# Weight stream of a 32-expert layer: order of the low part's products, place of the down biases, one more raw buffer

## The chip, the core and the metric

One core of a Trainium2 chip runs the whole program. The metric is the device time of one execution in microseconds (us), the median of several runs. The engines have their own instruction queues: PE (TensorE, matrix products), DVE (VectorE), ACT (ScalarE), POOL (GpSimd, here mostly the issuer of indirect transfers) and SP (SyncE, the issuer of the weight loads). An instruction waits for semaphores at the head of its engine's queue, and what stands behind it waits with it.

## The reference

512 tokens of width 1024 pass through a first block (retention and pooling, an expert layer, an embedding gate) and a second block of attention. The change touches the expert layer alone:

```python
def moe(hn, router_w, router_b, w_gu, b_gu, w_down, b_down):
    logits = xt @ router_w + router_b
    top_vals, top_idx = lax.top_k(logits, TOP_K)
    gates = jax.nn.softmax(top_vals, axis=-1)
    ...
    gu = lax.ragged_dot(xs, w_gu, group_sizes) + b_gu[sorted_e]
    gate = jnp.minimum(gu[:, ::2], SWIGLU_LIMIT)
    up = jnp.clip(gu[:, 1::2], -SWIGLU_LIMIT, SWIGLU_LIMIT)
    act = (up + 1.0) * (gate * jax.nn.sigmoid(SWIGLU_ALPHA * gate))
    y = lax.ragged_dot(act, w_down, group_sizes) + b_down[sorted_e]
    y = y * gates[order]
    out = jnp.zeros_like(xt).at[tok].add(y)
```

Everything is in fp32. The weights of an expert are 1024x2048 (gate and up) and 1024x1024 (down), 12 MB, 384 MB for all 32: each is read once.

## The kernel before

**Precision.** A product in fp32 is made of products of a coarser type, fp32r. A weight tile is split in a high part (`wh`, a copy on ACT, L937) and a low part (`wl`, raw minus high, on DVE, L938). The token matrix is split likewise (`xh`, `xl`). The product is xh·wh + xl·wh + xh·wl.

**Tiles.** `chunks` walks an expert's three 1024x1024 matrices (the gate_up halves 0 and 1, down) in row tiles of 128x1024: 8 for a matrix, 24 for an expert, 768 in all. One load of 1 MB, issued by SP through `load` (L167), brings two tiles into the next raw buffer of the ring `self.wr`: `wr` (2 buffers), `wr2` (3) and two halves of the residual's buffer `self.h`, seven in all. A load waits until the two tiles that the buffer held have been split. Six pairs of buffers hold high and low parts in turn (`parts`).

**Two kinds of experts.** Sixteen experts (0, 1, 3, 5, ... 29) have room for 96 tokens, and xh and xl are separate operands: six matmuls of 96 rows by 512 columns a tile, in the helper `mm3` (L187 xh·wh, L188 xl·wh, L189 xh·wl), first for the bank of columns 0 to 511, then for that of 512 to 1023. The other sixteen (2, 4, ... 30, 31) have room for 64, and xh and xl stand side by side in one operand of 128 columns: four matmuls a tile (L942). The diff leaves these as they are. The two kinds are streams of their own (`stream`), which the loop at the end of `moe` takes in turn, a tile of each, once the stream of the first kind has a lead of 24 tiles; so the last 24 tiles are of the second kind alone.

**Side work.** What isn't a product of weights runs as jobs: generators that are stepped between tiles, each saying after how many tiles it wants its next step. `fetch` gathers an expert's tokens (POOL, `xg`) and transposes them, `clamped` and `folded` apply the activation, `out` scales the result (ACT, `ys`) and adds it to `y_d` in memory by an indirect transfer of POOL (L1028). All additions into `y_d` come one after the other, each when the one before has landed. `finish` runs a job to its end at once where its result is needed. Jobs share two PSUM banks named `tr`; `bank()` hands them out.

**The down biases.** `gated_bias` adds gates times `b_down` to all 512 tokens, 128 at a time (t = 0 to 3): a transpose of the gates, two matmuls of 512 columns, two copies on ACT into `yb` (L1148), and an indirect addition of 512 KB into `y_d` (L1150). Its job starts at the many-token expert 11. There is one buffer `yb`, which the raw bias rows (`bd`) use first.

**The start.** `early` issues the first loads before the router's tables are ready: seven into the ring, then, behind the branch that deals with overflowing experts (`overflow`), an eighth into the result buffer `ys`. After the last tile, `y_d` is read back (L1265) and the embedding gate follows, then the attention block.

Of the kernel before, what the change touches and what calls it, by code (L numbers as in the profile page):

```python
# [9 lines left out]
F32 = mybir.dt.float32  # L10
F32R = mybir.dt.float32r
# [3 lines left out]
AF = mybir.ActivationFunctionType  # L15
ALU = mybir.AluOpType
# [3 lines left out]
D = 1024  # L20
# [122 lines left out]
class Kern:  # L143
# [189 lines left out]
    def run(self):  # L333
        tc, nc, I = self.tc, self.nc, self.I
        with ExitStack() as g:
            self.con = g.enter_context(tc.tile_pool(name="con", bufs=1))
            self.dr = g.enter_context(tc.tile_pool(name="dr", bufs=1, space=bass.MemoryType.DRAM))
            self.h = self.con.tile([128, NT, D], F32, name="h")
            self.hn_d = self.dr.tile([S, D], F32, name="hn_d")
            self.y_d = self.dr.tile([S, D], F32, name="y_d")  # L340
            self.x2_d = self.dr.tile([S, D], F32, name="x2_d")
            wr = g.enter_context(tc.tile_pool(name="wr", bufs=2))
            wh = g.enter_context(tc.tile_pool(name="wh", bufs=2))
            with ExitStack() as a:
                wr2 = a.enter_context(tc.tile_pool(name="wr2", bufs=3))
                self.wr = [wr2, wr, wr2, wr, wr2]
                self.wh = [wh] * 2
                self.rp = a.enter_context(tc.tile_pool(name="rp", bufs=1))
                self.junk = self.rp.tile([128, D], BF16, name="junk")
                with ExitStack() as f:  # L350
                    self.front(f)
                with ExitStack() as f:
                    Q = f.enter_context(tc.tile_pool(name="mq", bufs=2, reuse_waits="tile"))
                    self.wr = [wr, wr2, wr, wr2, wr2] + [Part(self.h[:, 2 * i:2 * i + 2, :]) for i in range(2)]
                    self.moe(f, Q)
                self.wr, self.wh = [wr], [wh]
            with ExitStack() as f:
                self.back(f)
# [449 lines left out]
    def moe(self, f, Q):  # L808
# [115 lines left out]
        def chunks(src, ps, pair, raw=(), bias=None, few=False):  # L924


            if bias is not None and not few:
                for n in range(2):
                    bias(n, True)
            for c0 in range(0, 8, 2):  # L930
                w = raw.pop(0) if raw else self.load(src(c0 * 128, 256).rearrange("o (k p) n -> p (o k) n", p=128), 2, 1024)
                for kk in range(2):
                    k = c0 + kk
                    hi, lo = self.next(parts)
                    if raw:
                        nc.vector.tensor_copy(hi[:, 0:1], tabs[0][1])
                    nc.scalar.activation(hi, w[:, kk], AF.Copy)  # L937
                    nc.vector.tensor_tensor(out=lo, in0=w[:, kk], in1=hi.bitcast(F32), op=ALU.subtract)  # L938
                    if few:
                        for part in (hi, lo):  # L940
                            for n in range(2):
                                nc.tensor.matmul(ps[:, n, :], pair[2][:, k, :], part[:, n * 512:n * 512 + 512],  # L942
                                                 start=k == 0 and part is hi, stop=k == 7 and part is lo)
                                if bias is not None and k == 0 and part is hi:
                                    bias(n, False)
                    else:
                        for n in range(2):
                            nn = slice(n * 512, n * 512 + 512)
                            self.mm3(ps[:, n, :], (pair[0][:, k, :], pair[1][:, k, :]), (hi[:, nn], lo[:, nn]),
                                     bias is None and k == 0, k == 7)  # L950
                    yield k

        def pieces(src, ps, pair, first, last):
# [162 lines left out]

        def gated_bias():

            bd = T.tile([128, D], F32, tag="yb", name="bd", bufs=1)
            for r in range(0, 128, NE):  # L1120
                nc.sync.dma_start(bd[r:r + NE], I["expert_b_down"][0])
            bs = P.tile([128, D], F32R, name="bs")
            yield 8
            nc.scalar.activation(bs, bd, AF.Copy)
            nc.vector.tensor_tensor(out=bs[64:128], in0=bd[64:128], in1=bs[64:128].bitcast(F32), op=ALU.subtract)
            rows = P.tile([128, NT], I32, name="rows")
            for t in range(NT):
                g4 = T.tile([128, 4, NE], F32, tag="g4", name="g4", bufs=1)
                nc.vector.tensor_copy(g4, self.G[:, t, None, :].to_broadcast([128, 4, NE]))
                nc.vector.tensor_scalar(rows[:, t:t + 1], c["far"], 128.0 * t - FAR - 1, None, op0=ALU.add)  # L1130
                yield 1
                tp, free = yield from bank()
                nc.tensor.transpose(tp[:, 0:128], g4.rearrange("p a e -> p (a e)"), c["ident"])
                yield LAG
                gT = T.tile([128, 128], F32R, tag="gT", name="gT", bufs=1)
                nc.scalar.activation(gT, tp[:, 0:128], AF.Copy)
                yield 1
                for r in (32, 96):
                    q = slice(r, r + NE)
                    nc.vector.tensor_tensor(out=gT[q], in0=tp[q, 0:128], in1=gT[q].bitcast(F32), op=ALU.subtract)  # L1140
                free()
                yield 1
                y = T.tile([128, D], F32, tag="yb", name="yb", bufs=1)
                for n in range(2):
                    ps, free = yield from bank()
                    nc.tensor.matmul(ps, gT, bs[:, n * 512:n * 512 + 512], start=True, stop=True)
                    yield LAG
                    nc.scalar.activation(y[:, n * 512:n * 512 + 512], ps, AF.Copy)  # L1148
                    free()
                nc.gpsimd.indirect_dma_start(out=self.y_d[:, :], out_offset=bass.IndirectOffsetOnAxis(ap=rows[:, t:t + 1], axis=0),  # L1150
                                             in_=y, in_offset=None, bounds_check=S - 1, oob_is_err=False, compute_op=ALU.add)
                yield 8

        ne = self.ne
        self.gates(self.G[:, :, 0:2], self.tcols0, 2, T)
# [11 lines left out]
            nc.sync.dma_start(dst, self.wsrc(wgu[i // 8], 2 * (i % 4), 2, 1024 * (i // 4 % 2), 1024))  # L1167
            return dst

        raws = [early(i, self.next(self.wr).tile([128, 2, 1024], F32, tag="wr", name="wr")) for i in range(7)]  # L1170
        overflow()
        raws.append(early(7, ys))

        def stream(es):

            for e, after in zip(es, es[1:] + [None]):
# [2 lines left out]
                    J[after, "x"] = job(fetch(after, 16))  # L1179
                if not LESS[e] and 4 * (at // 2) + 4 in BATCHES and at % 2 == 0:  # L1180
                    job(table(4 * (at // 2) + 4))
                if e == 11:
                    job(gated_bias())
                yield from gate_up(e, 0)
                if at and after is not None:
                    yield from down(es[at - 1])
                yield from gate_up(e, 1)
            for e in es[-2:]:
                yield from down(e)
# [494 lines left out]
```

## Time and profile before

| | |
|---|---|
| median of 3 runs | 1834.57 us (1832.08 to 1838.57) |
| profiled run | 1836.86 us |
| its span, first to last instruction | 1835.0 us |
| mean granted clock of TensorE | 0.981 of full speed |
| busy share of the span | PE 95%, DVE 83%, ACT 65%, POOL 12% |
| weights and other data read | 470.90 MB |

The profile is one execution. Its stages: up to about 250 us the first block's mixing, the router and the tables; to about 1362 us the expert stream; then the embedding gate and the attention. Busy times of PE are modelled and overlap, so a busy PE is not one at its peak. The DMA share is the mean busy share of the 16 DMA engines, and it can pass 1.00 a little. The granted clock is TensorE's, as a share of 2.4 GHz; its two levels are 1.2 and 2.4.

### The profile page before, as it was taken

Reading aid. Unit: us, or ns where it says so; the run is one execution under the profiler, and the core shown is the slowest. Engines: PE = TensorE matmul, PEld = TensorE weight load, DVE = VectorE, ACT = ScalarE, POOL = GpSimd, SP = SyncE. Lnnn points to the kernel's source line nnn. Section 1 sums busy time; section 2 is a strip of 40 time slices with the busy share of each in tenths; the row PEclk is TensorE's granted clock in tenths of the full one; section 3 lists DMA queues with packets and bytes.
Section 4 is the critical chain, followed back from the end, with each engine's and each line's share of the span. In section 5 each row is a group of like instructions: output and inputs, shape, how many; then the busy total and the mean of one; then the engine's idle time right before and its main releaser. Section 6 shows DMA issues by size and latency. Waiting matters only on the chain. (4 is left out here: it accounts for less than half of the span.)

```text
span 1835.0 us, 24671 instructions
## 1 busy us (share of the span) xinstructions
PE 1739.8 (95%) x8375; PEld 1285.0 (70%) x8379; DVE 1529.2 (83%) x2665; ACT 1193.9 (65%) x1591; POOL 221.2 (12%) x124
## 2 busy tenths in 40 slices
PE   8999779999999998999999999999978999999999
PEld 6887657666776775766666666766656777787776
DVE  5574589999999998999999999999977769999542
ACT  5224258778878777887788788788875445554431
POOL 0011212131111311210201211110310000000000
PEclk9999879999999998999999999999999999999999
DMA  8224469999999999999999999999985222201211
GB/s 283 85 95 149 147 219 354 384 354 389 378 391 386 373 379 363 341 391 383 379 374 393 384 371 395 383 382 391 391 291 188 91 63 82 89 28 53 84 54 40
DMA packets 148295, 493.18 MB, mean 269 GB/s; under 512 B 14369, under 2 KB 18721, under 8 KB 148160
## 3 DMA queue, kind: packets, MB, share of 16 engines
q1 hardware_dynamic: 137600, 462.02, 67.1%
q0 software_dynamic: 8640, 24.78, 6.0%
q10 hardware_dynamic: 1920, 4.72, 0.7%
q8 instruction: 68, 1.11, 0.2%
q14 instruction: 67, 0.55, 0.1%
HBM read 470.90 MB, written 25.17 MB: 270 GB/s over the span
## 5 line engine op out<-in xcount | busy, mean ns | idle before, releaser
L938 DVE TENSOR_TENSOR wl<-wr,wh 128x1024 fp32r<-128x1024 f32 x550 | 641.8, 1215 | 30.9 <-ACT wh L937 30.1
L937 ACT ACTIVATE wh<-wr 128x1024 fp32r<-128x1024 f32 x550 | 544.1, 1050 | 46.3 <-DMA wr<-in_expert_w_gate_up_dram 19.0
L938 DVE TENSOR_TENSOR wl<-h,wh 128x1024 fp32r<-128x1024 f32 x216 | 252.9, 1215 | 13.8 <-ACT wh L937 13.8
L189 PE MATMUL mm<-wl,x 128*96 128x512 f32 x512 | 208.6, 407 | 16.9 <-DVE wl L938 15.9
L937 ACT ACTIVATE wh<-h 128x1024 fp32r<-128x1024 f32 x216 | 214.9, 1050 | 14.6 <-DMA h<-in_expert_w_gate_up_dram 7.3
L187 PE MATMUL mm<-wh,x 128*96 128x512 f32 x512 | 206.0, 402 | 0.7 <-ACT x L239 0.4
L188 PE MATMUL mm<-wh,x 128*96 128x512 f32 x512 | 203.2, 397 | 0.0
L1028 POOL DMA_INDIRECT y_d<-ys,gi x48 | 116.9, 2435 | 640.5 <-ACT ys L1026 390.8
L942 PE MATMUL mm<-wl,x 128*128 128x512 f32 x512 | 169.8, 412 | 1.4 <-DVE wl L938 1.2
L942 PE MATMUL mm<-wh,x 128*128 128x512 f32 x512 | 168.1, 399 | 3.1 <-ACT wh L937 3.1
L189 PEld LDWEIGHTS mm<-wl,x 128*96 128x96 f32 x512 | 82.9, 162 | 72.5 <-DVE wl L938 41.1
L189 PE MATMUL mm<-wl,a 128*96 128x512 f32 x256 | 103.9, 406 | 15.1 <-DVE wl L938 15.0
L942 PEld LDWEIGHTS mm<-wh,x 128*128 128x128 f32 x512 | 96.2, 189 | 31.2 <-ACT wh L937 4.0
L187 PE MATMUL mm<-wh,x2h 128*128 128x512 f32 (+2 forms) x288 | 114.6, 398 | 0.3 <-ACT x2h L239 0.3
L188 PE MATMUL mm<-wh,x2l 128*128 128x512 f32 (+2 forms) x288 | 111.3, 387 | 0.0
L189 PE MATMUL mm<-wl,x2h 128*128 128x512 f32 (+2 forms) x288 | 111.0, 387 | 0.1
L942 PEld LDWEIGHTS mm<-wl,x 128*128 128x128 f32 x512 | 89.0, 189 | 29.7 <-DVE wl L938 13.2
L181 DVE TENSOR_TENSOR wl<-wr,wh 128x2048 fp32r<-128x2048 f32 (+3 forms) x40 | 76.6, 1915 | 36.7 <-ACT wh L180 36.5
L188 PEld LDWEIGHTS mm<-wh,x 128*96 128x96 f32 x512 | 83.6, 163 | 33.3 <-DVE x L241 0.4
L187 PEld LDWEIGHTS mm<-wh,x 128*96 128x96 f32 x512 | 83.2, 163 | 31.3 <-ACT wh L937 3.5
L890 POOL DMA_INDIRECT xg<-hn_d,gi x32 | 67.6, 2114 | 291.4 <-PE tr L905 229.5
L187 PE MATMUL mm<-wh,a 128*96 128x512 f32 x256 | 102.2, 399 | 0.0
(437 smaller groups left out, 3271.2 us busy)
## 6 DMA issues: line engine op xcount, KB each, us to landing
wr<-in_expert_w_gate_up_dram SPq DMA_DIRECT2D x184, 1024.0 KB, 12.6
wr<-in_expert_w_down_dram SPq DMA_DIRECT2D x91, 1024.0 KB, 13.0
h<-in_expert_w_gate_up_dram SPq DMA_DIRECT2D x71, 1024.0 KB, 11.9
h<-in_expert_w_down_dram SPq DMA_DIRECT2D x37, 1024.0 KB, 13.5
wr<-in_w_in_dram SPq DMA_DIRECT2D x20, 1024.0 KB, 5.1
wr<-in_w_out_dram SPq DMA_DIRECT2D x8, 1024.0 KB, 4.9
wr<-in_ple_gate_w_dram SPq DMA_DIRECT2D x4, 1024.0 KB, 5.3
wr<-in_w_in_dram SPq DMA_DIRECT2D x4, 512.0 KB, 5.6
```

Of the source, the lines that this page charges most:

```text
L181: nc.vector.tensor_tensor(out=lo[:, sl], in0=raw[:, sl], in1=hi[:, sl].bitcast(F32), op=ALU.subtract)
L187: mm(out, a[0], b[0], start=first, stop=False)
L188: mm(out, a[1], b[0], start=False, stop=False)
L189: mm(out, a[0], b[1], start=False, stop=last)
L890: nc.gpsimd.indirect_dma_start(out=xgs[LESS[e]][0:m], out_offset=None, in_=self.hn_d[:, :], in_offset=bass.IndirectOffsetOnAxis(ap=tabs[e] ...
L937: nc.scalar.activation(hi, w[:, kk], AF.Copy)
L938: nc.vector.tensor_tensor(out=lo, in0=w[:, kk], in1=hi.bitcast(F32), op=ALU.subtract)
L942: nc.tensor.matmul(ps[:, n, :], pair[2][:, k, :], part[:, n * 512:n * 512 + 512], start=k == 0 and part is hi, stop=k == 7 and part is lo)
L1028: nc.gpsimd.indirect_dma_start(out=self.y_d[:, :], out_offset=bass.IndirectOffsetOnAxis(ap=rows[0:m // n], axis=0), in_=y[o:o + m // n], i ...
```

## The change

1. A many-token tile's six matmuls come in another order: xh·wh for both banks, xl·wh for both, xh·wl for both. The low part is first wanted by the fifth matmul instead of the third.
2. `gated_bias` starts at the last but one many-token expert (27), between its two gate_up halves, instead of at expert 11. It has no buffers of its own: `yb` is a slot of the `a96` ring (the second operand of a many-token expert), and the split bias rows and the four transposed gates (`bs`, `gT`) share a slot of the `x96` ring (its first operand). All four transposes go into one `tr` bank and are copied out at once. Pauses between steps are shorter. `yb` is still one buffer for the four additions.
3. A pool `wr4` adds an eighth raw buffer to the ring. Eight early loads go into the ring, a ninth into `ys`.

```diff
-                    self.wr = [wr, wr2, wr, wr2, wr2] + [Part(self.h[:, 2 * i:2 * i + 2, :]) for i in range(2)]
+                    more = f.enter_context(tc.tile_pool(name="wr4", bufs=1, reuse_waits="tile"))
+                    self.wr = [wr, wr2, wr, wr2, wr2, more] + [Part(self.h[:, 2 * i:2 * i + 2, :]) for i in range(2)]
...
                     else:
-                        for n in range(2):
-                            nn = slice(n * 512, n * 512 + 512)
-                            self.mm3(ps[:, n, :], (pair[0][:, k, :], pair[1][:, k, :]), (hi[:, nn], lo[:, nn]),
-                                     bias is None and k == 0, k == 7)
+                        for x, part in ((pair[0], hi), (pair[1], hi), (pair[0], lo)):
+                            for n in range(2):
+                                nc.tensor.matmul(ps[:, n, :], x[:, k, :], part[:, n * 512:n * 512 + 512],
+                                                 start=bias is None and k == 0 and x is pair[0] and part is hi, stop=k == 7 and part is lo)
...
         def gated_bias():
-            bd = T.tile([128, D], F32, tag="yb", name="bd", bufs=1)
+            y = T.tile([128, 1536], F32, tag=f"a{CAP}", name="yb")[:, 0:D]
+            bs = T.tile([128, 1536], F32R, tag=f"x{CAP}", name="bs")
+            gT, bs = bs[:, D:1536], bs[:, 0:D]
             for r in range(0, 128, NE):
-                nc.sync.dma_start(bd[r:r + NE], I["expert_b_down"][0])
-            bs = P.tile([128, D], F32R, name="bs")
-            yield 8
-            nc.scalar.activation(bs, bd, AF.Copy)
...
+            tp, free = yield from bank()
+            for t in range(NT):
+                g4 = T.tile([128, 4, NE], F32, tag="g4", name="g4")
...
+                nc.tensor.transpose(tp[:, self.tok(t)], g4.rearrange("p a e -> p (a e)"), c["ident"])
+            yield LAG
+            nc.scalar.activation(gT, tp, AF.Copy)
+            nc.scalar.activation(bs, y, AF.Copy)
...
+            for t in range(NT):
                 for n in range(2):
                     ps, free = yield from bank()
-                    nc.tensor.matmul(ps, gT, bs[:, n * 512:n * 512 + 512], start=True, stop=True)
-                    yield LAG
+                    nc.tensor.matmul(ps, gT[:, self.tok(t)], bs[:, n * 512:n * 512 + 512], start=True, stop=True)
+                    yield 3
                     nc.scalar.activation(y[:, n * 512:n * 512 + 512], ps, AF.Copy)
                     free()
                 nc.gpsimd.indirect_dma_start(out=self.y_d[:, :], out_offset=bass.IndirectOffsetOnAxis(ap=rows[:, t:t + 1], axis=0),
                                              in_=y, in_offset=None, bounds_check=S - 1, oob_is_err=False, compute_op=ALU.add)
-                yield 8
+                yield 5
...
-        raws = [early(i, self.next(self.wr).tile([128, 2, 1024], F32, tag="wr", name="wr")) for i in range(7)]
+        raws = [early(i, self.next(self.wr).tile([128, 2, 1024], F32, tag="wr", name="wr")) for i in range(8)]
         overflow()
-        raws.append(early(7, ys))
+        raws.append(early(8, ys))
...
-                if e == 11:
-                    job(gated_bias())
                 yield from gate_up(e, 0)
                 if at and after is not None:
                     yield from down(es[at - 1])
+                if not LESS[e] and at == len(es) - 2:
+                    job(gated_bias())
                 yield from gate_up(e, 1)
```

On PE a tile of an expert with many tokens stood like this before (`wh` and `wl` are the tile's high and low part, `x` the tokens' operand):

```order
L187 MATMUL mm<-wh,x 96x512
L188 MATMUL mm<-wh,x 96x512
L189 MATMUL mm<-wl,x 96x512
L187 MATMUL mm<-wh,x 96x512
L188 MATMUL mm<-wh,x 96x512
L189 MATMUL mm<-wl,x 96x512
```

and stands like this now, two tiles in a row:

```order
L950 MATMUL mm<-wh,x 96x512 x4
L950 MATMUL mm<-wl,x 96x512 x2
L950 MATMUL mm<-wh_1903,x 96x512 x4
L950 MATMUL mm<-wl_1904,x 96x512 x2
L950 MATMUL mm<-wh_1905,x 96x512 x4
```

The two products with the low part moved from third and sixth place to fifth and sixth.

POOL's indirect transfers at the stream's end before (`y_d<-ys` is the addition of an expert's result, `xg` a gather of tokens; the last eleven additions belong to experts 25 to 31):

```order
L890 DMA xg_1893<-hn_d,gi 64x1024
L890 DMA xg_1892<-hn_d,gi 96x1024
L1028 DMA y_d<-ys,gi 512x1024 x3
L890 DMA xg_1893<-hn_d,gi 64x1024
L1028 DMA y_d<-ys,gi 512x1024 x11
```

and now, with the four biases' additions (`y_d<-yb`):

```order
L891 DMA xg_1896<-hn_d,gi 64x1024
L1029 DMA y_d<-ys,gi 512x1024 x3
L1153 DMA y_d<-yb,rows 512x1024 x2
L1029 DMA y_d<-ys,gi 512x1024 x2
L1153 DMA y_d<-yb,rows 512x1024 x2
L1029 DMA y_d<-ys,gi 512x1024 x6
```

The biases' additions, which stood one by one among those of the middle experts, now stand in two pairs with two of an expert between them, six additions before the end.

ACT near the second of these pairs now (`yb` the copies of a bias, `ys` an expert's result, `gs` and `ag` the activation, `a` an operand of down):

```order
L1000 ACTIVATE gs<-mm 128x1024
L938 ACTIVATE wh<-wr 128x1024
L239 ACTIVATE a<-tr 128x4x96 x2
L938 ACTIVATE wh_1903<-wr 128x1024
L1027 ACTIVATE ys<-mm,gt 96x1024
L1151 ACTIVATE yb<-tr 128x512
L938 ACTIVATE wh<-wr 128x1024
L938 ACTIVATE wh_1905<-wr 128x1024
L973 ACTIVATE ag<-ag 128x256
L938 ACTIVATE wh<-wr 128x1024 x2
L1151 ACTIVATE yb<-tr 128x512 x2
L938 ACTIVATE wh<-h 128x1024 x2
```

The first `yb` row is the second half of the third bias, the pair the two halves of the fourth: five instructions lie between the one and the next, which overwrites the buffer that the third's addition reads.

SP's queue before the tables, before the change:

```order
L1167 DMA wr<-in_expert_w_gate_up_dram 128x2x1024 x2
L574 DMA wp<-in_pool_w_dram 128x4x128
L1167 DMA wr<-in_expert_w_gate_up_dram 128x2x1024 x3
L1167 DMA h<-in_expert_w_gate_up_dram 128x2x1024 x2
L1121 DMA bd<-in_expert_b_down_dram 32x1024 x2
```

and with it:

```order
L1170 DMA wr<-in_expert_w_gate_up_dram 128x2x1024 x2
L575 DMA wp<-in_pool_w_dram 128x4x128
L1170 DMA wr<-in_expert_w_gate_up_dram 128x2x1024 x4
L1170 DMA h<-in_expert_w_gate_up_dram 128x2x1024 x2
L1040 TENSOR_LOAD order
```

One load of 1 MB is added to the early ones, and the bias rows are gone from there.

## Rows read from the trace of the kernel before

**Rows 1.** The page, first part: busy us (share of the span) and instructions of each engine.

```profile
PE 1739.8 (95%) x8375; PEld 1285.0 (70%) x8379; DVE 1529.2 (83%) x2665; ACT 1193.9 (65%) x1591; POOL 221.2 (12%) x124
```

**Rows 2.** All engines, 425 to 675 us: busy (instructions), granted clock, DMA share, GB/s.

```profile
425.00:675.00 250.00, 241.56 (x1123) 171.56 (x1123) 238.08 (x295) 201.72 (x234) 44.61 (x18) 1.00 1.02 385
```

**Rows 3.** Three windows, `wl` (L938) alone: DVE busy (x count), clock, DMA share, GB/s.

```profile
425.00:675.00 250.00, 202.91 (x175) 1.00 1.02 385
675.00:925.00 250.00, 188.84 (x162) 0.98 1.02 370
925.00:1175.00 250.00, 203.22 (x176) 1.00 1.02 384
```

**Rows 4.** Transfers, 425 to 675 us: queue: packets, MB, share of 16 engines' time.

```profile
q1 hardware_dynamic: 23689, 91.33, 93.6%
q0 software_dynamic: 1566, 4.59, 8.4%
```

**Rows 5.** Transfers, 675 to 925 us: queue: packets, MB, share of 16 engines' time; issues.

```profile
q1 hardware_dynamic: 22193, 85.56, 89.5%
q0 software_dynamic: 2272, 6.76, 12.5%
...
y_d<-yb,rows POOLq DMA_INDIRECT x4, 9.7
```

**Rows 6.** Transfers, 925 to 1175 us: queue: packets, MB, share of 16 engines' time.

```profile
q1 hardware_dynamic: 23779, 91.69, 94.2%
q0 software_dynamic: 1552, 4.13, 7.4%
```

**Rows 7.** Timeline from 688 us: start, us, engine, line; in brackets idle time and releaser.

```profile
688.08 0.40 PE L187 MATMUL mm<-wh,x 128*96 128x512 f32 x1
...
688.31 0.39 PE L188 MATMUL mm<-wh,x 128*96 128x512 f32 x1
...
690.23 0.60 ACT L1148 ACTIVATE yb<-tr 128x512 f32<-128x512 f32 x1 [4.25 <-DMA y_d<-yb,rows]
...
691.81 2.36 DVE L938 TENSOR_TENSOR wl<-wr,wh 128x1024 fp32r<-128x1024 f32 x2 [3.87 <-ACT wh L937]
...
691.83 1.22 PE L942 MATMUL mm<-wh,x 128*128 128x512 f32 x2 [2.90 <-ACT wh L937]
```

**Rows 8.** All engines in the slice of 10 us that holds this wait.

```profile
690.00:700.00 10.00, 8.17 (x25) 5.55 (x26) 5.95 (x7) 6.54 (x11) 1.71 (x2) 0.56 1.03 399
```

**Rows 9.** The biases' scatter-adds (L1150): from issue to landing.

```profile
DMA to landing us min/median/max: 9.7/9.7/10.6
```

**Rows 10.** All engines, two windows near the stream's end.

```profile
1300.00:1340.00 40.00, 39.95 (x185) 29.57 (x184) 37.15 (x38) 34.14 (x39) 13.28 (x3) 1.00 1.03 401
1350.00:1355.00 5.00, 4.44 (x17) 2.51 (x16) 5.00 (x7) 3.68 (x6) 0.00 (x0) 1.00 0.68 235
```

**Rows 11.** Timeline, the last `wl` of the stream (L938).

```profile
1355.82 6.90 DVE L938 TENSOR_TENSOR wl<-wr,wh 128x1024 fp32r<-128x1024 f32 x6 [0.32 <-ACT wh L937]
```

**Rows 12.** All engines, two windows around the stream's start.

```profile
225.00:250.00 25.00, 10.21 (x48) 7.03 (x49) 18.24 (x68) 9.49 (x11) 2.04 (x2) 0.50 0.38 121
275.00:300.00 25.00, 25.00 (x120) 18.36 (x119) 25.00 (x28) 22.03 (x27) 2.56 (x1) 1.00 1.00 344
```

**Rows 13.** Timeline of SyncE's (SP) issues before and behind the overflow branch.

```profile
240.41 0.39 SPq L167 DMA_DIRECT2D wr<-in_expert_w_gate_up_dram  x1
250.15 0.39 SPq L1167 DMA_DIRECT2D ys<-in_expert_w_gate_up_dram  x1
```

**Rows 14.** Waits, 300 to 1350 us: engine and line, waited for: us in total, times, longest.

```profile
PE mm L189 <- DVE wl L938: 31.0, 70, 1.1
```

**Rows 15.** Timeline of POOL: first and last of the last four scatter-adds.

```profile
1355.11 1.68 POOL L1028 DMA_INDIRECT y_d<-ys,gi  x1 [20.65 <-ACT ys L1026]
...
1375.96 1.41 POOL L1028 DMA_INDIRECT y_d<-ys,gi  x1 [3.33 <-DMA y_d<-ys,gi]
```

More of the change, by code (lines that the diff above doesn't have):

```diff
@@ L1125, in gated_bias @@
-            nc.vector.tensor_tensor(out=bs[64:128], in0=bd[64:128], in1=bs[64:128].bitcast(F32), op=ALU.subtract)
+                nc.sync.dma_start(y[r:r + NE], I["expert_b_down"][0])
             rows = P.tile([128, NT], I32, name="rows")
             for t in range(NT):
-                g4 = T.tile([128, 4, NE], F32, tag="g4", name="g4", bufs=1)
+                nc.vector.tensor_scalar(rows[:, t:t + 1], c["far"], 128.0 * t - FAR - 1, None, op0=ALU.add)
+            tp, free = yield from bank()
@@ L1129, in gated_bias @@
+            for t in range(NT):
+                g4 = T.tile([128, 4, NE], F32, tag="g4", name="g4")
                 nc.vector.tensor_copy(g4, self.G[:, t, None, :].to_broadcast([128, 4, NE]))
-                nc.vector.tensor_scalar(rows[:, t:t + 1], c["far"], 128.0 * t - FAR - 1, None, op0=ALU.add)
                 yield 1
-                tp, free = yield from bank()
-                nc.tensor.transpose(tp[:, 0:128], g4.rearrange("p a e -> p (a e)"), c["ident"])
-                yield LAG
-                gT = T.tile([128, 128], F32R, tag="gT", name="gT", bufs=1)
@@ L1136, in gated_bias @@
[L1136 to L1143, printed above, removed]
+                nc.tensor.transpose(tp[:, self.tok(t)], g4.rearrange("p a e -> p (a e)"), c["ident"])
@@ new lines, in gated_bias @@
+            yield LAG
+            nc.scalar.activation(gT, tp, AF.Copy)
+            nc.scalar.activation(bs, y, AF.Copy)
+            yield 1
+            for r in (32, 96):
+                q = slice(r, r + NE)
+                nc.vector.tensor_tensor(out=gT[q], in0=tp[q], in1=gT[q].bitcast(F32), op=ALU.subtract)
+            free()
+            yield 1
+            nc.vector.tensor_tensor(out=bs[64:128], in0=y[64:128], in1=bs[64:128].bitcast(F32), op=ALU.subtract)
+            yield 1
+            for t in range(NT):
@@ L1144, in gated_bias @@
                 for n in range(2):
                     ps, free = yield from bank()
-                    nc.tensor.matmul(ps, gT, bs[:, n * 512:n * 512 + 512], start=True, stop=True)
-                    yield LAG
+                    nc.tensor.matmul(ps, gT[:, self.tok(t)], bs[:, n * 512:n * 512 + 512], start=True, stop=True)
+                    yield 3
                     nc.scalar.activation(y[:, n * 512:n * 512 + 512], ps, AF.Copy)
```

## The prediction

> **What bounds the kernel now.** I read the page's engine table first. The matmul engine PE is busy 95% of the span, the vector engine DVE 83%, the scalar engine ACT 65% [rows 1]. These are averages over stages, so I went to windows of the expert stream, where all the diff's edits lie. In an undisturbed stretch of 250 us there, PE is busy 241.6 us, DVE 238.1 us, and the 16 DMA engines have a share of 1.02 at 385 GB/s [rows 2]. Three resources are within 5% of full at once, so a term that relieves only one of them deserves distrust.
>
> The pace comes from counting the one DVE instruction that every 128-row weight tile needs (the low part, `wl`): 175, 162 and 176 of them in three neighbouring stretches of 250 us [rows 3]. That is 1.42 to 1.43 us a tile in the first and third, and 13 or 14 tiles too few in the middle. The transfers tell it more finely: the hardware queue q1, which carries the weights, moved 91.33 MB in the first, 85.56 in the middle and 91.69 in the third [rows 4 to 6]. The four scatter-adds of the down bias lie in the middle one.
>
> How full PE really is cannot be told from its busy share, since its matmuls overlap: each is drawn as 0.39 or 0.40 us, but in a run of them they start 0.23 us apart [rows 7]. Six of them make 1.4 us for a tile of an expert with many tokens, four make 0.9 for one with few, 1.16 in the mean of the two, and a tile takes 1.42. The rest is transposes, folding and waits.
>
> **Term 1, the biases leave the middle.** The deficit of the middle stretch is (91.33 + 91.69)/2 - 85.56 = 5.95 MB of weights; at 91.5 MB per 250 us that is 16.3 us. It has two parts. The software queue q0, which carries gathers and scatters, took 12.5% of the engines' time there and 8.4% and 7.4% in the neighbours [rows 4 to 6]: 4.6% of 250 us is 11.5 us of transfer time, 2.9 us for each of the four [rows 5]. The other 4.8 us is a stall. The second bias's copy on ACT waits 4.25 us for the first bias's scatter, because there is one buffer `yb`; behind it in ACT's order stand the high parts `wh`, so DVE waits 3.87 us and PE 2.90 us [rows 7], and the granted clock falls to 0.56 of full speed for that slice of 10 us [rows 8], near the lower of its two levels. A scatter-add takes 9.7 us to land [rows 9]. The change takes all of this out of the stretch: -16.3 us. One tile more or less at each edge is 1.4 us, so the bounds are -14 and -19.
>
> **Term 2, the biases arrive near the end.** Their job now starts between the two halves of expert 27, and the eight copies into `yb` stand where, by the order of the changed program, some 84 to 34 of the 768 tiles are left. The transfers cost 11.5 us there too. But the end has slack in the transfers: DMA falls to 0.68 after 1350 us [rows 10], where I take it the last weights have landed, while DVE works tiles off almost without a break until 1355.82 + 6.90 = 1362.7 us [rows 11]. So the last load could come some 10 us later, and by term 1 it comes 16.3 us sooner. Hence I let DMA hide the 11.5 us. What DMA can't hide is ACT's order. There is again one `yb` for four biases. In the changed order the third bias's first half stands a few instructions behind the second bias's scatter, and the fourth's first half likewise behind the third's; the first two lie far enough apart to hide most of one landing. I price these two by the stall that the trace shows, 4.25 us each, 8.5 in all. DVE runs at 37.15 of 40 us near the end [rows 10], so it can win back about 7% of what follows, under 3 us in the last 40; the copy of the bias rows, which takes a buffer that expert 27's first matmuls still read, and expert 29's operand, whose buffer is held longer, cost about as much. I take +8.0. The bounds are 0 (slack hides both stalls) and +20 (two stalls and the 11.5 us of transfers).
>
> **Term 3, the eighth raw buffer.** Between 225 and 250 us the tables are made and DMA is busy 0.38 [rows 12]. SyncE issues one load at 240.41, then sits in the branch on overflowing experts, and the next, into `ys`, goes at 250.15 [rows 13]. In the changed order a further load of 1 MB is among those issued before that branch, and the loads of the bias rows that stood there are gone. It arrives in idle time, so the saturated stage has one load of 1.0486 MB less to bring: at 0.366 MB/us that is -2.9 us; I take -2.7; the 0.4 MB of bias rows that now come within the stream fall into the slack of term 2. The opening (275 to 300 us) has DVE at 25.00 of 25 us and DMA at 344 GB/s, below its later rate [rows 12]: there DVE sets the pace and a longer ring only stores the gain. That a longer ring also evens out the middle I put at nothing, because DMA's share is 1.02 there already. Bounds 0 and -6.
>
> **Term 4, the low part's products last.** A tile's `wl` is now wanted by the fifth of six matmuls, not the third: two spacings, 0.46 us, later. The trace charges 31.0 us in 70 waits of PE to `wl`, 0.44 us in the mean and none over 1.1 [rows 14], so most of this wait should go. But DVE, which makes `wl`, is 95% busy, and the raw data come at the pace of DMA: a PE that waits less here waits for `wh` or for a raw tile instead. I count 0, with bounds -10 (a third of the wait) and +2 (the planner places other work a tile later). A rule of the Trainium skill stands against any gain: "Perfetto Trace Analysis", section on the most-contended engine, says that the busy share of matmuls does not tell how near PE is to its limit; the spacing of 0.23 us beside durations of 0.39 agrees, and by the rule this term is 0 too.
>
> Elsewhere nothing moves that matters: the attention block keeps its instructions, and after the stream the last scatters go one after the other, from 1355.11 to 1375.96 us [rows 15]; in the changed order the biases' last stands six scatters before the end, so it should have landed before that chain begins.
>
> **The sum.** The profiled run took 1836.9 us (span 1835.0 and 1.9 outside). 1836.9 - 16.3 + 8.0 - 2.7 + 0 = 1825.9. The median of the runs, 1834.6, is 2.3 us under the profiled one, so the forecast is 1823.6. Its own range is 1814 to 1830.
>
> **Rivals.** *The biases only change place.* If DMA is the limit from 300 us to the end, its time is conserved: 11.5 us of transfers and 4.8 of stall come back, and only the early load stays won: 1836.9 - 2.7 - 2.3 = 1831.9, no measurable change. For it: a share above 1 in the stretches of [rows 3]. Against it: DVE ends 12 us after the transfers thin out [rows 10, 11], so the end isn't DMA's.
>
> *The end stalls decide, and it is slower.* The scatter-adds of POOL run one after the other, each waiting for the landing of the one before; near the end those of experts 26 to 28 crowd in between. A bias scatter that waits its turn there makes ACT wait a whole landing of 9.7 us [rows 9] twice, 19.4 us, and each wait costs the clock of a slice as at 690 us, 10 x 0.44 = 4.4 us more. With nothing to win it back: 1836.9 - 16.3 - 2.7 + 19.4 + 8.8 - 2.3 = 1843.8. It is slower than before once the end's stalls and their clock exceed 19 us. Against it: by the places in ACT's order the waits begin some way into the landing, as the old one did.
>
> *Reorder and ring lift the whole stream.* In 1300 to 1340 us, with few gathers or scatters near, DMA reaches 401 GB/s [rows 10], 4% above 385. If PE's waits and the ring's length are what keeps it lower, half of that over the 925 us from 425 to 1350 is 18 us: 1823.6 - 18 = 1805.6. For it: PE's 31 us of waits for `wl`. Against it: the share of 1.02, which leaves nothing to lift unless it counts waiting packets. The Trainium skill ("DMA: Bandwidth & Descriptors", section Bandwidth) gives some 358 GB/s as the limit from memory for a core and 435 as that of the fabric; the trace's 385 and 401 lie above the first, so it doesn't hold here, and below the second, which would leave this rival room.
>
> **How the numbers follow.** Forecast 0.53, only a change of place 0.22, slower by the end's stalls 0.13, whole stream faster 0.12. A difference of 0.3% is 5.5 us, about what a measurement of this kernel can tell from no change: faster is below 1829.1, slower above 1840.1. Of the forecast's 0.53 some 0.04 lies within 0.3%, of the second case 0.03 below it and 0.01 above: faster 0.53 - 0.04 + 0.12 + 0.03 = 0.64, same 0.22 - 0.04 + 0.04 = 0.22, slower 0.13 + 0.01 = 0.14. For eight in ten I leave out half of the slow case and half of the fast one and a little of each tail: 1806 to 1838.
>
> **What would show it.** Term 1: in the profile after, no 250 us of the stream with under 90 MB of weights, and no clock below 1.00 in the middle. Term 2: two waits of ACT at `yb` for the biases' scatters near the end, 4 to 5 us each; if 9 or more, the slow rival. If transfers thin out less than 5 us before DVE's last `wl`, DMA set the end and the second case is right. Term 3: one more load issued before 230 us. Term 4: PE's waits for `wl` well below 31 us with the pace per tile unchanged; a pace under 1.40 us in the stretches without biases would make the third rival right and my zero wrong.

## The result, and the profile after

The changed kernel is slower: 1846.32 us in the median of 6 runs (1843.6 to 1849.36) against 1834.36 us for the kernel before (6 runs beside them). The ratio is 1.0065, with an interval of 1.0047 to 1.0082, that is 12 us more where 11 us less were forecast. The profiled run took 1845.32 us with a span of 1843.2, so the two profiled runs lie 8.5 us apart where the medians lie 12.

The first view is the one of [rows 3], the low parts `wl` counted by windows (columns: length, DVE busy and count, granted clock, DMA share, GB/s), here of the kernel after:

```profile
425.00:675.00 250.00, 202.56 (x175) 1.00 1.02 379
675.00:925.00 250.00, 198.14 (x171) 1.00 1.02 384
925.00:1175.00 250.00, 202.30 (x175) 1.00 1.02 384
1175.00:1350.00 175.00, 129.69 (x112) 0.96 1.01 362
```

and the last of these windows before:

```profile
1175.00:1350.00 175.00, 144.85 (x125) 1.00 1.02 389
```

The middle stretch has 171 tiles where it had 162: nine are won, 13 us. The stretches on both sides of it, where the biases never were, have about as many as before (175 and 175, against 175 and 176). The last 175 us have 112 where they had 125: thirteen are lost.

The transfers say the same of the three long windows, if a little less well (queue q1: packets, MB, share), in the order of time, to be compared with [rows 4 to 6]:

```profile
q1 hardware_dynamic: 23347, 90.01, 93.5%
```

```profile
q1 hardware_dynamic: 23613, 91.04, 93.9%
```

```profile
q1 hardware_dynamic: 23689, 91.33, 93.7%
```

The middle gained 5.5 MB and the two others lost 1.7 together. So no stretch of the stream got faster than an undisturbed one was before, and two got slower by a hair.

What happened in the last window is in ACT's timeline (start, us, instruction; in brackets idle time and releaser) and POOL's:

```profile
1260.82 0.60 ACT L1151 ACTIVATE yb<-tr 128x512 f32<-128x512 f32 x1 [4.24 <-DMA y_d<-yb,rows]
1309.11 0.59 ACT L1151 ACTIVATE yb<-tr 128x512 f32<-128x512 f32 x1
1322.72 0.60 ACT L1151 ACTIVATE yb<-tr 128x512 f32<-128x512 f32 x1 [8.17 <-DMA y_d<-yb,rows]
```

```profile
1290.94 15.20 POOL L1029 DMA_INDIRECT y_d<-ys,gi  x1 [6.12 <-DMA y_d<-ys,gi]
1312.74 2.03 POOL L1153 DMA_INDIRECT y_d<-yb,rows  x1 [6.60 <-ACT ag L973]
1325.08 1.57 POOL L1153 DMA_INDIRECT y_d<-yb,rows  x1 [10.30 <-ACT yb L1151]
```

ACT waits twice at `yb`, as the prediction said, but 4.24 and 8.17 us, 12.4 in all. The second wait is long because the third bias's addition, ready at 1309.7 when its second half is copied, is issued only at 1312.74, behind the two of expert 28; ACT, which stands at the next `yb` soon after, waits for its issue and its landing. The second of those two took 21.1 us from issue to landing, 15.20 of them in POOL's own instruction, where the first had taken 1.40. What makes it so long stays open. One of the same kind stands ahead of the long wait in e1 below (14.56 us), and one in e12 (15.20 us), where no copy waits for it. In the time of the second wait everything behind ACT runs dry (all engines, as in [rows 8]):

```profile
1320.00:1330.00 10.00, 6.63 (x18) 4.80 (x19) 4.22 (x5) 6.39 (x9) 1.57 (x1) 0.56 0.86 262
```

DVE works 4.2 of 10 us, the clock falls to 0.56, and DMA's share to 0.86, as no raw buffer comes free. The stream's last `wl` ends 8.1 us later than in [rows 11]:

```profile
1368.46 2.36 DVE L939 TENSOR_TENSOR wl<-h,wh 128x1024 fp32r<-128x1024 f32 x2
```

The waits of the whole stream (300 to 1350 us: engine and line, waited for, us in total, times, longest) show a second change. Before:

```profile
ACT a L239 <- PE tr L988: 22.9, 19, 2.3
...
DVE ag L970 <- PE mm L189: 12.3, 7, 1.8
```

After:

```profile
ACT a L239 <- PE tr L989: 61.1, 25, 3.1
...
DVE ag L971 <- PE mm L950: 37.0, 27, 1.6
...
PE mm L943 <- DVE wl L939: 11.3, 26, 1.0
PE mm L950 <- DVE wl L939: 10.6, 26, 0.7
```

PE's waits for `wl` in many-token tiles fell from 31.0 us [rows 14] to 10.6, and 11.3 came up in the few-token tiles (3.2 us before). Two other waits grew about threefold: DVE at the clamp of a many-token half (`ag`), for PE's last product of that half, 12.3 to 37.0 us; and ACT at the copy of the down operand (`a`), for PE's transposes, 22.9 to 61.1.

### The profile page after: what moved, and what is told of

The parts are those of the page before. It is cut to its first block, busy times and chain, and to the rows that moved or that the text cites. A ratio compares the mean times of both kernels' runs of the same rounds, so it can differ in the third digit from the quotient of the medians.

```text
span 1843.2 us, 24641 instructions
## 1 busy us (share of the span) xinstructions
PE 1748.7 (95%) x8378; PEld 1280.2 (69%) x8379; DVE 1528.1 (83%) x2661; ACT 1188.9 (65%) x1588; POOL 217.8 (12%) x124
## 4 chain that ended last, share of the span: by engine, by line
PE 53%; DVE 19%; issue 6%; DMA 5%; ACT 4%; POOL 0%; SPq 0%; DVEq 0%; POOLq 0%; ACTq 0%
PE mm L950 20%; PE mm L943 12%; DVE wl L939 9%; PE mm L187 4%; PE mm L188 3%; PE mm L189 3%; ACT wh L938 2%; DMA y_d<-ys,gi 2%; PE po L1503 2%; PE tr L227 2%; PE tr L1007 2%; DMA y_d<-yb,rows 2%; PE mm L1052 1%; PE tr L1586 1%; DVE isc L1449 1%
## 5 line engine op out<-in xcount | busy, mean ns | idle before, releaser
L939 DVE TENSOR_TENSOR wl<-wr,wh 128x1024 fp32r<-128x1024 f32 x576 | 672.0, 1216 | 23.0 <-ACT wh L938 23.0
L938 ACT ACTIVATE wh<-wr 128x1024 fp32r<-128x1024 f32 x576 | 567.0, 1047 | 39.4 <-DMA wr<-in_expert_w_gate_up_dram 19.0
L950 PE MATMUL mm<-wh,x 128*96 128x512 f32 x1024 | 283.7, 398 | 2.5 <-ACT wh L938 1.1
L939 DVE TENSOR_TENSOR wl<-h,wh 128x1024 fp32r<-128x1024 f32 x190 | 222.9, 1215 | 13.9 <-ACT wh L938 13.6
L938 ACT ACTIVATE wh<-h 128x1024 fp32r<-128x1024 f32 x190 | 188.9, 1049 | 2.6 <-DMA h<-in_expert_w_gate_up_dram 1.2
L950 PE MATMUL mm<-wl,x 128*96 128x512 f32 x512 | 163.9, 401 | 1.6 <-DVE wl L939 1.2
L950 PE MATMUL mm<-wh,a 128*96 128x512 f32 x512 | 141.8, 397 | 0.7 <-ACT gs L1000 0.7
L950 PEld LDWEIGHTS mm<-wh,a 128*96 128x96 f32 x512 | 82.5, 163 | 34.2 <-ACT gs L1000 1.1
L943 PE MATMUL mm<-wl,a 128*128 128x512 f32 x256 | 93.1, 437 | 4.8 <-DVE wl L939 4.3
L180 ACT ACTIVATE wh<-wr 128x2048 fp32r<-128x2048 f32 (+3 forms) x40 | 64.5, 1616 | 45.9 <-PE mm L188 41.0
## 6 DMA issues: line engine op xcount, KB each, us to landing
h<-in_expert_w_down_dram SPq DMA_DIRECT2D x32, 1024.0 KB, 10.9
```

Of the source, the lines that this page charges most:

```text
L180: nc.scalar.activation(hi[:, sl], raw[:, sl], AF.Copy)
L950: nc.tensor.matmul(ps[:, n, :], x[:, k, :], part[:, n * 512:n * 512 + 512], start=bias is None and k == 0 and x is pair[0] and part is hi, ...
```

## The experiments

All times are medians, each beside runs of the kernel before on the same chip (1833.7 to 1834.1 us there). Theories: **P**, the place of the biases near the end is what costs; **R**, the reorder or the ring slows the stream; **F**, the job's new form does. Later, **Q** and **O** split R, and **T** is on transfers.

**e1_mid: the changed kernel with the biases at expert 11.**

```diff
-                if not LESS[e] and at == len(es) - 2:
+                if e == 11:
                     job(gated_bias())
```

> The changed kernel with one line moved: the bias job starts at expert 11 again (between its two halves), in its new form, with the reorder and the eighth buffer kept. Before is 1834.4 us, after 1846.3. Theory P (the place of the biases near the end is what costs): the loss goes away, and the early load stays won, 1829 to 1834. Theory R (reorder or ring slow the stream, as the 1.3 MB fewer weights in 425 to 675 us might say): 1838 or more. Theory F (the job's new form, which borrows operand buffers, costs wherever it stands): 1840 or more, with waits of ACT for an operand near 700 us.

Measured: 1850.8 us, ratio 1.0092 (1.0076 to 1.0108). P falls as it was put: back at the old place the changed kernel is slower still. Its waits name the reason:

```profile
ACT yb L1151 <- DMA y_d<-yb,rows: 17.1, 1, 17.1
```

One copy waited 17.1 us, again for a bias's addition that stood in POOL's queue behind three additions of experts, one of them the long one of 14.56 us. So not the place but the wait for the one `yb` looked to be the price. R and F, which both allowed this time, are told apart by the next three runs.

**e2_reorder: the kernel before with the new order of the matmuls alone.**

```diff
-                        for n in range(2):
-                            nn = slice(n * 512, n * 512 + 512)
-                            self.mm3(ps[:, n, :], (pair[0][:, k, :], pair[1][:, k, :]), (hi[:, nn], lo[:, nn]),
-                                     bias is None and k == 0, k == 7)
+                        for x, part in ((pair[0], hi), (pair[1], hi), (pair[0], lo)):
+                            for n in range(2):
+                                nc.tensor.matmul(ps[:, n, :], x[:, k, :], part[:, n * 512:n * 512 + 512],
...
```

> The kernel before with the new order of the six matmuls alone. Theory P: 1833 to 1836, no change, PE's waits for the low part in many-token tiles well under 31 us. Theory R: 1838 to 1842. The rival of the prediction by which the whole stream gets faster: 1815 to 1825.

Measured: 1841.26 us, ratio 1.0041 (1.0026 to 1.0055): 7.5 us slower, with nothing else changed. R holds for the order. (ACT's wait at `yb` is 6.0 us here for 4.3 before, so by the table below some 1.7 of the 7.5 us may be the biases'.) The two waits are there already:

```profile
ACT a L239 <- PE tr L988: 55.5, 28, 3.1
...
DVE ag L970 <- PE mm L949: 36.1, 27, 1.6
```

**e3_noreorder: the changed kernel with the old order.** Its diff is that of e2, reversed, on the changed kernel.

> The changed kernel with the old order of the six matmuls, everything else as changed. Theory P: 1845 to 1848, as the changed kernel. Theory R, if it is the order that costs: 1836 to 1842.

Measured: 1836.23 us, ratio 1.0018 (1.0009 to 1.0028): 10.1 us less than the changed kernel, only 2.5 above the one before, where P had 1845 to 1848. The middle stretch here has 174 tiles for the 162 of [rows 3], and the last 175 us 114 for 125.

**e4_end7: the kernel before with the bias job near the end alone.** Seven raw buffers, old order, one buffer for the gates (`g4`) instead of two, and for the job, against the changed kernel:

```diff
-            y = T.tile([128, 1536], F32, tag=f"a{CAP}", name="yb")[:, 0:D]
-            bs = T.tile([128, 1536], F32R, tag=f"x{CAP}", name="bs")
-            gT, bs = bs[:, D:1536], bs[:, 0:D]
+            y = T.tile([128, D], F32, tag="yb", name="yb", bufs=1)
+            bs = P.tile([128, D], F32R, name="bs")
+            gT = P.tile([128, 512], F32R, name="gT")
```

> The kernel before with the bias job near the end alone: its new start, steps and pauses, but buffers of its own, seven raw buffers, and the old order of the matmuls. Theory P: 1846 to 1850 (the changed kernel, and 2.7 for the early load that is missing). Theory R: 1834 or less, since neither reorder nor eighth buffer is there. Theory F: 1838 to 1843, as expert 29's operand isn't held up.

Measured: 1853.9 us, ratio 1.0102 (1.0078 to 1.0125), 4 us above what P gave it and the slowest of all. Its buffers are its own, so F isn't the reason. Three copies waited at `yb`, 24.6 us in all, one of them 15.28:

```profile
1312.06 0.60 ACT L1150 ACTIVATE yb<-tr 128x512 f32<-128x512 f32 x1 [15.28 <-DMA y_d<-yb,rows]
```

With the same place and the same order of matmuls e3 has 9.9 us in one wait. Why the copies meet POOL's queue so differently in the two wasn't tried apart.

**e6_before_nobias and e8_nobias8: what the biases and the ring cost.** Both leave out the four additions of the down bias; the second also has the eighth raw buffer and the ninth early load.

```diff
-                if e == 11:
-                    job(gated_bias())
```

> The kernel before without the job of the down biases: the four additions of gates times b_down are left out, nothing else. Theory P, term 1 of the prediction: 16.3 us less than before, 1816 to 1820. If DMA has no part and only the stall of ACT counts: 1828 to 1830. If the transfers are hidden and the stall is made up later: 1833 or more.

> The same without the biases (they are left out again), and with the eighth raw buffer and the ninth early load, which now have room. Term 3 of the prediction: 2.7 us less than the run without biases and seven buffers, 1813 to 1818. The rival by which a longer ring lifts the whole stream: 8 us or more less than that run. A ring that brings nothing: within 1 us of it.

Measured: 1820.65 us, ratio 0.9918 (0.9897 to 0.9938), and 1819.72 us, ratio 0.9918 (0.9898 to 0.9938). The biases cost the kernel before 13.4 us by the medians, 15 by the ratio, close to the 16.3 that term 1 read from the trace. The eighth buffer brings 0.9 us, no difference that can be measured.

**e9_pinned and e13_pins_old: why the new order costs.** The places in the engines' queues are set before the kernel runs, by a scheduler. The trace of the changed kernel suggested (Q) that with the new order it sets the clamp and the copies of the down operand closer to the matmuls that they wait for. The traces bear this out: counted by the `wl` ahead of it on DVE, the clamp stands two weight tiles earlier in e2 than before in 20 of the 32 many-token halves and at the same place in the others; the first of the copies stands 1.8 tiles earlier on ACT in the mean. Two one-column copies tie both to later places, once with the new order and once with the old:

```diff
+            nc.vector.tensor_copy(gt[:, 0:1], parts[-3][1][0:CAP, 0:1].bitcast(F32))
             clamp(gu[:, :, 0], gu[:, :, 1])
...
             yield LAG
+            nc.scalar.activation(p[0][:, 4 * half, 0:1], parts[-2][0][:, 0:1].bitcast(F32), AF.Copy)
             for which in "hl":
```

> The kernel before with the new order of the matmuls, and the side work of a many-token half held back: a one-column copy on DVE that reads an earlier low part ties the clamp to a later place in DVE's queue, one on ACT does so for the first copies of the down operand. Theory Q (the new order costs because the clamp and those copies now stand some two tiles closer, in DVE's and ACT's queues, to the matmuls that they wait for): waits of DVE for the last product under 5 us, of ACT for the transposes under 25 us, and 1832 to 1837. Theory O (the order of the matmuls costs by itself): the waits go, the time stays at 1840 to 1845.

> The kernel before, old order of the matmuls, with the same two one-column copies that held the side work back in the run before last: their own price. If they cost 2 to 4 us (1836 to 1838), as 32 copies of 0.15 us on DVE and of 0.20 us on ACT and the later places might, then the new order has no price left once the side work stands later (theory Q whole). If they cost nothing or help (1831 to 1835), the new order keeps 2 to 5 us of its own (Q in part, O for the rest).

Measured: 1837.04 us with the new order, ratio 1.0017 (1.0004 to 1.003), and 1839.21 us with the old one, 1.0034 (1.0021 to 1.0048). In the first the wait of DVE at the clamp for PE's last product is no longer in the list, and that of ACT for PE's transposes is down to one:

```profile
ACT a L239 <- PE tr L989: 1.9, 1, 1.9
```

The ties cost the old order 5.4 us, so later places are no gain in themselves: they set the clamp two tiles and the copies 6 to 18 tiles later than before, and ACT's wait for DVE at those copies grew, from 8.8 us before to 35.6 in e13 and from 2.5 in e2 to 18.4 in e9. But with the clamps at the same places in both, the new order is 2.2 us below the old one, no difference that can be measured, where it was 7.5 above. What it costs goes away when those two waits do: Q. O, a price of the order itself, finds no support. In e9 3.0 of the 7.5 us are left; that these are the ties' own price is read from e13 and not shown by itself, as the ties shift other work too.

**e12_twoyb_old: the late biases without ACT's waits.** Old order, seven raw buffers, and two `yb` in turn for the room of the eighth.

```diff
-            y = T.tile([128, 1536], F32, tag=f"a{CAP}", name="yb")[:, 0:D]
+            y = T.tile([128, D], F32, tag="yb", name="yb", bufs=2)
...
                 nc.gpsimd.indirect_dma_start(out=self.y_d[:, :], ...
+                y = T.tile([128, D], F32, tag="yb", name="yb", bufs=2)
                 yield 5
```

> The changed kernel's place and form of the biases with the old order of the matmuls, two buffers yb in turn, and for the room seven raw buffers as before. No copy of a bias should wait for a landing. Theory P (ACT's waits at yb are what the end costs): 1818 to 1827. Theory T (the 11.5 us of transfers come back at the end, with or without waits): 1829 to 1834. If the shared buffer of the first operand or the place costs by itself: 1838 or more, as the run with the place alone (1853.9) would say if its one yb weren't the cause.

Measured: 1829.23 us, ratio 0.9977 (0.9963 to 0.9991). This is the one kernel that beats both, by 4.8 us the one before (by the ratio 4.2) and by 17 the one after, though less than 0.3%. So P, with 1818 to 1827, falls short, and the time lies at the lower end of T's 1829 to 1834. No copy of a bias waits for a landing any more, the clock stays at 1.00, and the last 175 us have 121 tiles for the 112 of the changed kernel. It still costs 8.6 us more than no biases at all. It borrows the first operand's buffer as the changed kernel does, so that part of F costs nothing that shows. ACT's waits near the end are now for weights:

```profile
1314.29 2.01 ACT L937 ACTIVATE wh<-h 128x1024 fp32r<-128x1024 f32 x2 [2.01 <-DMA h<-in_expert_w_down_dram]
...
1326.91 2.01 ACT L937 ACTIVATE wh<-wr 128x1024 fp32r<-128x1024 f32 x2 [2.01 <-DMA wr<-in_expert_w_gate_up_dram]
...
1336.42 2.01 ACT L937 ACTIVATE wh<-h 128x1024 fp32r<-128x1024 f32 x2 [2.08 <-DMA h<-in_expert_w_down_dram]
```

From 1175 to 1360 us ACT waits 14.1 us for the experts' weights at `wh`; without biases (e6) it is 3.1, and with the new order 11.8 (e7) against 1.0 (e5). So once the stalls are gone, the weights come late at the end when the additions are there: T. That all of the 8.6 us is time of the transfers, and none the engines' work for the biases, isn't shown.

**e7_twoyb: the same with the new order.** It is the kernel just shown, with the order of the changed one's matmuls.

> The changed kernel with two buffers yb and seven raw ones: the new order kept, no ACT wait for a landing. If the prices add, 1829.2 for the same with the old order and 7 to 10 for the new one: 1836 to 1840. If the new order costs nothing beside late biases without stalls: 1827 to 1832.

Measured: 1836.31 us, ratio 1.0012 (1.0001 to 1.0024). The new order costs 7.1 us here too; the prices add.

**e5_after_nobias: the changed kernel without its biases.** The additions are left out, the rest is as changed.

> The changed kernel without the biases' additions (they are left out): new order, eight raw buffers. By the sum of the runs so far, 1819.7 for eight buffers without biases and 7.5 to 10 for the new order: 1826 to 1831; the biases near the end would then cost the changed kernel 15 to 20 us. If the new order costs only with the stalls of the biases around: 1819 to 1823.

Measured: 1825.41 us, ratio 0.9954 (0.9938 to 0.997), 5.7 above e8: the new order costs without any biases around as well. The biases cost the changed kernel 1846.3 - 1825.4 = 20.9 us, where they had cost 13.4.

**e14_opening: the biases where DMA was thought to have room.**

```diff
-                if e == 11:
+                if e == 1:
                     job(gated_bias())
```

> The kernel before with the bias job started at expert 1 instead of 11, otherwise its old form: the additions fall into 260 to 400 us, where DVE sets the pace at first and transfers have room. Theory T (the biases' transfers cost 2.9 us each wherever DMA is full, and nothing where it isn't; waits of ACT come on top): 1821 to 1828. If DVE's own work for them counts there instead (some 5 us): 1827 to 1832. If the place doesn't matter: 1832 to 1836.

Measured: 1833.54 us, ratio 1.0004 (0.9992 to 1.0015), no change. A miss for T as I put it: the copies of the biases never wait for a landing, yet the biases cost 12.9 us. Three of the four additions fall between 250 and 425 us, the fourth at 484.8. From 250 to 425 us the stream makes 111 tiles for 117 (the kernel before first, then e14):

```profile
250.00:425.00 175.00, 135.84 (x117) 1.00 1.00 357
```

```profile
250.00:425.00 175.00, 130.24 (x111) 0.99 1.00 343
```

DMA's share is 1.00 in both over this stretch, and ACT waits 7.8 us for weights in e14, where the kernel before has no such wait; so the room wasn't there. How much of the six tiles is transfers and how much DVE's own work for the biases stays open.

**The price of the biases, put together.** For each kernel: how long ACT waited at `yb` in its profiled run, and its median less that of the run without biases with the same order (1820.65 with seven raw buffers, 1819.72 with eight, 1825.41 with eight and the new order).

| kernel | waits at `yb`, us | price, us |
|---|---|---|
| e12, near the end, two `yb` | 0 | 8.6 |
| e7, the same, new order | 0 | 10.9 |
| e14, opening | 0 | 12.9 |
| before, expert 11 | 4.3 | 13.4 |
| e3, near the end, old order | 9.9 | 16.5 |
| after, near the end | 12.4 | 20.9 |
| e1, expert 11, new form | 17.1 | 25.4 |
| e4, near the end, own buffers | 24.6 | 33.2 |

The three kernels without a wait pay 8.6 to 12.9 us, which differ by place, form and order. From the lowest of them, 8.6 us and one more for each us of waiting gives 12.9, 18.5, 21.0, 25.7 and 33.2 for the last five rows, within 2 us of each. From 12.9 the five would come out some 4 to 6 us too high, and between e14 and the kernel before, which differ in the place alone, 4.3 us of waiting make only 0.5 us. So "one for one" is a fit to these rows, good to some 4 us, and not a law. (The waits are those of one profiled run each, the prices are differences of medians; e7 has seven raw buffers and is set against a run with eight, which by e6 and e8 is within 1 us.)

## Why the prediction was wrong

**Term 1 held, at its lower edge.** I took 16.3 us for the biases in the middle, 11.5 of transfers and 4.8 of stall. Left out, they give back 13.4, just under my bound of 14 (15 by the ratio, within it), and the middle stretch gained 9 tiles with the new order, 12 with the old (e3), for the 11 or 12 that 16.3 us would be.

**Term 2 failed, in two steps, and weighs most.** The term was +8.0; measured, the same biases cost 20.9 us near the end. The first step that failed is "I let DMA hide the 11.5 us". It rested on a slack of some 10 us: I took DMA's fall to 0.68 after 1350 us [rows 10] for the landing of the last weights. It wasn't. In the kernel before, the last of the experts' loads was issued at 1344.41 us, and this is its time to landing (the row of the loads issued from 1335 us on):

```profile
wr<-in_expert_w_down_dram SPq DMA_DIRECT2D x4, 1024.0 KB, 13.4
```

So the last weights landed at 1357.8 us, 4.9 us before the last `wl` ends at 1362.7 [rows 11], and the split of the two tiles that they bring (about 1 us of ACT and 1.2 us of DVE for each) takes most of these. There was next to no slack to hide anything in. Where no copy waits for a landing (e12), 8.6 us of the biases remain and ACT waits for weights, which land 3.6 us before the last `wl` ends. The second is the size of the stalls: I priced them at 4.25 us each by the one that the trace showed, and one was 8.17. That one had begun half way through a landing; here ACT also waits for POOL, which holds the addition back until the expert's before it have landed, the last of them after 21.1 us. My slow rival had this mechanism and asked for two full waits; one long wait was enough, since the transfers came back as well.

**Term 3 didn't show, and weighs little.** The extra load is issued where I said (four loads from 157.64 us where there were three). It brought 0.9 us for 2.7 (e6 and e8), and six runs of each can't tell this from nothing, nor well from 2.7. The rival of a longer ring that lifts the stream, 8 us or more, falls with it.

**Term 4 failed too, and weighs about half as much as term 2.** It stood at 0 with +2 as its worse bound; the new order costs 5.7 to 10.1 us in four comparisons, 7.5 in the plainest (e2), and an estimate that takes out the longer waits at `yb` leaves 5.7 to 7.6. The part on PE was right: its waits for `wl` in many-token tiles fell by two thirds, other waits took their place, and the stream got no faster by it. That the busy share says little of how near PE is to its limit was true and beside the point: the price came on DVE and ACT. What I passed over is the bound's own phrase, "the planner places other work a tile later". I had the changed order before me and compared places on PE and near the end, not how far the clamp and the operand's copies stand from the matmuls that they wait for. There DVE and ACT, in order, lost 24.7 and 38.2 us more to waits in the whole stream, and since `wl` and `wh` queue behind them, the tiles came later.

The sum by measured terms: 1834.1 - 13.4 (biases out of the middle) - 0.9 (ring) + 5.7 (order) + 20.9 (biases near the end) = 1846.4, for 1846.3 measured. Each term is the difference of two kernels in a row that leads from before to after, so this closes by construction; what it says is how far each was off: 12.9 us for term 2 (+20.9 for +8.0), 5.7 for term 4 (+5.7 for 0), 2.9 for term 1 and 1.8 for term 3, all to the same side.

**The rivals.** The one that came closest is the slow one, at 1843.8 us with a chance of 0.13; that it came so close is luck in part, as it had the stalls longer than they were and neither the transfers nor the new order's price. My check for term 2 ("4 to 5 us each; if 9 or more, the slow rival") lies between its two cases, 4.24 and 8.17. "Only change place" was right of the transfers, and what I held against it, that DVE ends 12 us after the transfers thin out, was the same misreading of the 0.68. By my other check (transfers thin out less than 5 us before the last `wl`) DMA didn't set the changed kernel's end: its last load landed at 1360.3 us, 10.5 before the last `wl` ends, as ACT's long wait had put everything behind it back. Before and in e12, with 4.9 and 3.6 us, the check says DMA.

## What to carry to other kernels

A buffer that is written again on an in-order engine while an indirect addition still reads it costs here about one us for every us of waiting there, and how long that is depends on what else stands in the issuer's queue; a second buffer was worth more here than another place for the work or an eighth raw buffer. Before counting a moved transfer as hidden, look up when the last load that the work needs lands: a share of the transfers that falls below 1 doesn't say that they are through. And a changed order of instructions is to be judged by what a scheduler does with everything around it: compare the distance between waiter and awaited on every engine, not only on the one that was edited.

## What the runs showed of the hardware

Waits of ACT of 4.3 to 24.6 us in all came through to the end about one for one (the table above, with its spread), in the middle of the stream as near its end, though ACT is busy only 65% of the span [rows 1]. A DMA share of about 1 said little of the rate: it was 1.00 at 343 GB/s from 250 to 425 us in e14, 1.00 at 357 in the same stretch before, and 1.02 at 389 from 1175 to 1350 us before. Nor did a fall of the share to 0.68 say that the last load had landed: that came after it, at 1357.8 us. POOL's instruction for an indirect addition into `y_d` took 1.4 to 2.5 us in four of five cases, and 13.3 to 15.2 us once or twice in 11 of the 14 traces, for a reason that stays open. The clock fell to 0.56 in the slice of a long wait, at 690 us before [rows 8] and at 1320 us after, and was back at 1.00 at the latest in the next slice but one.
